# Rotary products on VectorE, branch B's scores evacuated at raised priority, and pair 1's raw columns in general slots

## The chip, the cores and the metric

The kernel runs on one core of a Trainium2 chip. The metric is the device time of one execution in microseconds (us). The engines are TensorE (PE: matmuls, and PEld: the loading of their weights), VectorE (DVE), ScalarE (ACT), GpSimd (POOL) and SyncE (SP), which starts most DMA transfers. Each engine works through its own queue in order, and an instruction that waits for another engine holds up all that stand behind it.

## The reference, cut to what matters

Two layers over 1024 tokens of width 1024, all in float32. A layer projects its normalised input with one wide matrix, whose columns feed three token mixers and their gates. Branch A is a gated multiplication over chunks of tokens, branch C an attention without softmax. Branch B, which the change touches, is an attention over a sliding window with rotary q and k; the gates of all branches come from the same projection:

```python
h = rms_norm(x, g_pre)
p = h @ w_in                      # 7936 columns: u_a v_a gate_a q_b k_b v_b gate_b ... merge_logits
...
def rope(x, pos):
    x1, x2 = xf[..., :half], xf[..., half:]
    out = jnp.concatenate([x1 * cos - x2 * sin, x2 * cos + x1 * sin], axis=-1)
...
# branch B, blocks of 128 queries, each against its own and the previous block of 128 keys
s = jnp.einsum('bnqgrd,bnkgd->bngrqk', qb, kb) * (Dh ** -0.5)
s = jnp.where(valid, s, NEG)
p = jax.nn.softmax(jnp.concatenate([s, sink], axis=-1), axis=-1)[..., :-1]
o = jnp.einsum('bngrqk,bnkgd->bnqgrd', p, vb)
...
merged = gates_a * (y_a @ w_a) + gates_b * (y_b @ w_b) + gates_c * (y_c @ w_c)
x = x + rms_norm(merged @ w_out, g_post)
```

## The kernel before, in words

**Precision.** A float32 product is made of three matmuls on rounded operands (`mm3`, L128 to L130): each operand is split into a rounded part `hi` (ACT, L111) and a remainder `lo` (DVE, L112). A weight tile of 128 columns gives one cast `whi` (L111) and one subtraction `wlo` (L112) over 128x1024 elements.

**Order of the work.** The order on PE is that of the program, written out by hand. A list of projection jobs (`stream`) is dealt out in portions: `fill(us)` puts about so many microseconds of it between the steps of an attention, `need(label)` runs the list up to a job. The other engines' queues are set by a scheduler that takes the ready instruction of the highest priority; a block under `tc.high_priority()` goes ahead of work written before it. Tiles of 128x1024 live in 27 general slots, handed out first in, first out (`new`, `done`): a new tile waits for whatever still reads the slot's last tile. The numbers behind a name are slot and tile (s17_2701 is tile 2701 in slot 17).

**Branch B.** Columns of k (`kb`) and of four pairs of query heads (`qb0` to `qb3`) are projected in two halves each, evacuated by ACT (L279) and rotated (`rope`, L282): four transfers of 128 KB make a copy `sw` with halves exchanged (L292), POOL multiplies `sw` by sin (L293) and the tile `t` by cos (L294), DVE adds (L295). The result is split again (`after_q`: ACT L346, DVE L347, twice each). `scores(v)`, v from 0 to 7 and two for each query pair, makes 16 matmuls (L486) into two PSUM tiles `pz`, evacuates these by ACT (L492, L493, L498), a select on POOL (L494) and copies under a mask on DVE (L496, L499), and does the softmax: maximum (L503), small operations on 128x8 values (L504, L505, L509, L510), eight exponentials (ACT, L507) and a product (L511). The pool `pz` has two buffers, so the next `scores` waits for the evacuation of the last. Behind it stand transposes (L519, split by ACT L111 and DVE L112), selects (POOL, L526) and the product with v (L543, evacuated by ACT L553 and DVE L554). Before the first scores `fill(14)` stands, before the second `fill(3)`, before the loop `fill(FB[0])`; each step of the loop has more of them (FB[1] to FB[5]). The gate tiles of branch B (b0 to b3) are among the jobs dealt out; ACT takes the first half of each out of PSUM (L257), DVE the second (L253), into a general slot.

**Dense.** After the attentions the remaining projections run as block products with seven multiplications for a pair of column tiles (`dense`, L719). `begin(p)` loads the raw columns of pair p (two loads of 512 KB, L778), `prep(p)` makes seven operands `wop` of them (splits L111/L112, sums on POOL L751 to L762), `prod` multiplies. In odd pairs from the third on the raw columns stand in two general slots, in all others, pair 1 among them, in the two buffers of the pool `wr`, which the jobs' weights and pair 0 use as well. Branch A's normalisation (L615 to L621 on DVE) is issued at the start of `dense`.

Of the kernel before, what the change touches and what calls it, by code (L numbers as in the profile page):

```python
# [19 lines left out]
ALU = mybir.AluOpType  # L20
AX = mybir.AxisListType

P = 128
# [6 lines left out]
NEG = -1e30  # L30
# [3 lines left out]
O_M = 4864  # L34
NSLOT = 27
FC = (0.6, 0.6, 1.2, 0.6)
FB = (4, 1.5, 1.5, 1.8, 2.4, 2.4)
FB_MORE = {1: 2.3, 2: 1.3}


# [1 line left out]
def trunk(ctx, tc, x, w_in, gm_w_s, gm_b_s, gm_g, sinks, w_ba, w_bb, w_bc, b_merge, w_out,  # L42
          g_pre, g_post, cos_t, sin_t, out):
    nc = tc.nc
# [15 lines left out]
    def new(dt=F32):  # L60
        i = free.popleft()
        t = sp.tile([P, 1024], dt, name=f"s{i}", tag=f"s{i}", bufs=1)
        held[id(t)] = (i, t)
        return t

    def done(*ts):
        for t in ts:
            free.append(held.pop(id(t))[0])
# [72 lines left out]
    def step():  # L141

        while stream:
            j = stream[0]
            if j.gen is None:
                if j.w is None:
                    j.w = j.load()
                j.gen = j.run(j.w)
                if len(stream) > 1:
                    stream[1].w = stream[1].load()  # L150
            c = next(j.gen, None)
            if c is not None:
                for d in list(deferred):
                    d[0] -= c
                    if d[0] <= 0:
                        deferred.remove(d)
                        d[1]()
                return c
            finished.add(j.label)
            stream.popleft()  # L160
        return None

    def fill(us):
        while us > 0:
            c = step()
            if c is None:
                return
            us -= c

    def need(label):  # L170
        while label not in finished:
            assert step() is not None, label
# [72 lines left out]
    def queue_layer(l, S):  # L245
# [38 lines left out]
        def rope(t):  # L284
            if "cos" not in S:
                S["cos"], S["sin"] = new(), new()
                nc.sync.dma_start(S["cos"], cos_t)
                nc.sync.dma_start(S["sin"], sin_t)
            sw = new()
            for a in range(4):  # L290
                b = a ^ 1
                nc.sync.dma_start(sw[a * 32:(a + 1) * 32, :], t[b * 32:(b + 1) * 32, :])  # L292
            nc.gpsimd.tensor_tensor(sw, sw, S["sin"], op=ALU.mult)  # L293
            nc.gpsimd.tensor_tensor(t, t, S["cos"], op=ALU.mult)  # L294
            nc.vector.tensor_tensor(t, t, sw, op=ALU.add)  # L295
            done(sw)

# [173 lines left out]
    def branch_b(l, S):  # L471
        def scores(v):
            hp, nh = divmod(v, 2)
            grp = hp // 2
            need(("qb", hp))
            qT, kk = S["qs", hp], S["kk"][grp]
            s = new()
            s3 = s.rearrange("p (c k) -> p c k", c=8)
            for q in range(2):
                z = pz().rearrange("p (c k) -> p c k", c=4)  # L480
                for j in range(2):
                    n = nh * 4 + q * 2 + j
                    k0 = max(n - 1, 0) * P
                    for e in range(2):
                        for i in range(2):
                            nc.tensor.matmul(z[:, e * 2 + j], qT[e][:, n * P:(n + 1) * P], kk[i][:, k0:k0 + 256],  # L486
                                             start=i == 0, stop=i == 1)
                sq = s3[:, q * 4:(q + 1) * 4]
                mp = mprev.bitcast(I32).unsqueeze(1)
                if nh == 0 and q == 0:  # L490

                    nc.scalar.copy(sq[:, 0::2], z[:, 0::2, :P])  # L492
                    nc.scalar.copy(sq[:, 1::2], z[:, 1::2, P:])  # L493
                    nc.gpsimd.affine_select(sq[:, 0::2], sq[:, 0::2], pattern=[[0, 2], [-1, P]], compare_op=ALU.is_ge,  # L494
                                            fill=NEG, base=0, channel_multiplier=1)
                    nc.vector.copy_predicated(sq[:, 1::2], mp.to_broadcast([P, 2, P]), z[:, 1::2, :P])  # L496
                else:
                    nc.scalar.copy(sq, z[:, :, P:])  # L498
                    nc.vector.copy_predicated(sq, mp.to_broadcast([P, 4, P]), z[:, :, :P])  # L499
            mx = sm.tile([P, 8], F32, name="mx", tag="mx", bufs=3)  # L500
            ls = sm.tile([P, 8], F32, name="ls", tag="ls", bufs=3)
            es = sm.tile([P, 8], F32, name="es", tag="es", bufs=3)
            nc.vector.tensor_reduce(mx, s3, axis=AX.X, op=ALU.max)  # L503
            nc.vector.scalar_tensor_tensor(mx, mx, -1.0, nsnk8[:, l * 4 + hp], op0=ALU.mult, op1=ALU.min)  # L504
            nc.vector.tensor_tensor(es, mx, snk8[:, l * 4 + hp], op=ALU.add)  # L505
            for c in range(8):
                nc.scalar.activation(s3[:, c], s3[:, c], AF.Exp, bias=mx[:, c:c + 1], accum_out=ls[:, c:c + 1])  # L507
            nc.scalar.activation(es, es, AF.Exp)
            nc.vector.tensor_tensor(ls, ls, es, op=ALU.add)  # L509
            nc.vector.reciprocal(ls, ls)  # L510
            nc.vector.tensor_tensor(s3, s3, ls.unsqueeze(2).to_broadcast([P, 8, P]), op=ALU.mult)  # L511
            if nh:
                done(*qT)
            return s
# [44 lines left out]
                done(o)  # L559

        need(("qb", 0))
        fill(14)
        ready = {0: scores(0)}
        fill(3)
        ready[1] = scores(1)
        fill(FB[0])
        pend = None
        for v in range(8):
# [8 lines left out]
            if v >= 6:  # L577
                S["T"].go(3)
            fill(FB[1])
            if pend:  # L580
                attend(*pend)
            fill(FB[2])
            s = ready.pop(v)
            p0 = transp(s, 0)
            fill(FB[3] + FB_MORE.get(v, 0))
            p1 = transp(s, 1)
            done(s)
            if v >= 6:
                S["T"].go(3)
            fill(FB[4])  # L590
            attend(v, 0, p0, o)
            fill(FB[5])
            pend = (v, 1, p1, o)
# [125 lines left out]
    def dense(l, S):  # L719
# [45 lines left out]
        def begin(p):  # L765

            if p < len(pairs) and p not in begun:
                begun.add(p)
                raws[p] = ([], [])
                for q in range(2):  # L770
                    if p % 2 and p > 2:
                        t = new()
                        raws[p][1].append(t)
                        t = t.rearrange("p (k c) -> p k c", k=4)
                    else:
                        t = wp.tile([P, 4, 256], F32, name="wr", tag="wr", bufs=2)
                    col = pairs[p][0]
                    nc.sync.dma_start(t, w_in[l, q * 512:(q + 1) * 512, col:col + 256]  # L778
                                      .rearrange("(k p) c -> p k c", p=P))
                    raws[p][0].append(t)  # L780
# [303 lines left out]
    with tc.manual_schedule(engines={mybir.EngineType.PE}):  # L1084
# [3 lines left out]
        for l in range(L):  # L1088
            S = states[l]
# [49 lines left out]
```

## Time and profile before

| | us |
|---|---|
| median of 3 executions (2069.59 to 2070.36) | 2069.74 |
| the profiled execution | 2070.14 |
| its span, from the first instruction to the last | 2068.4 |
| PE busy | 2015.1 (97%) |
| DVE busy | 1227.0 (59%) |
| ACT busy | 808.3 (39%) |
| POOL busy | 504.3 (24%) |
| mean granted clock of PE | 0.989 of full speed |

The profiled execution lies 0.4 us above the median. Its time is 1.74 us more than its span, which is the time around the first and the last instruction. Busy times are sums over the span; a matmul's duration overlaps the next one's start, so the spacing of starts tells the pace of PE, not the durations. The granted clock is given as a share of 2.4 GHz, so 0.50 is 1.2 GHz. Times in the rows count from the start of the span.

### The profile page before, as it was taken

What the parts mean: (1) busy time and instruction counts of PE and PEld (TensorE: products, weight loads), DVE (VectorE), ACT (ScalarE), POOL (GpSimd) and SP (SyncE); (2) the same over time, 40 slices, a digit from 0 to 9 for tenths busy, and PEclk for the clock granted to TensorE, in tenths of its full rate; (3) what the DMA queues carried; (4) which work ended last, traced back from release to release, by engine and by line L of the source; (5) the groups of instructions that cost most, each with busy time, mean ns of one, the idle gap of its engine ahead of it and who ended that gap; (6) DMA issues with size and microseconds to landing.
All of it is one profiled execution on the core that took longest, in us unless ns stands there. A gap on an engine that the chain in (4) does not pass through costs nothing.

```text
span 2068.4 us, 26597 instructions
## 1 busy us (share of the span) xinstructions
PE 2015.1 (97%) x10193; PEld 1688.1 (82%) x10193; DVE 1227.0 (59%) x1609; ACT 808.3 (39%) x1477; POOL 504.3 (24%) x501
## 2 busy tenths in 40 slices
PE   7999998999999999999999999989989999999998
PEld 7898886897888888888898888779978888888886
DVE  5565638567676666554546565576766666655533
ACT  6344436543234434212444344455423343432221
POOL 0221223132433220151002222231344222202500
PEclk9999998999999999999999999989999999999999
DMA  7111232223466546632441112222235655476213
GB/s 237 39 42 42 82 82 72 88 82 116 156 232 202 178 138 244 232 124 92 135 130 31 42 41 83 75 78 101 89 99 201 226 186 169 152 254 224 82 52 132
DMA packets 169055, 261.81 MB, mean 127 GB/s; under 512 B 8616, under 2 KB 122336, under 8 KB 168928
## 3 DMA queue, kind: packets, MB, share of 16 engines
q1 hardware_dynamic: 162016, 234.95, 35.0%
q10 hardware_dynamic: 6912, 25.17, 3.0%
q8 instruction: 80, 1.31, 0.3%
q14 instruction: 47, 0.39, 0.1%
HBM read 175.15 MB, written 79.69 MB: 123 GB/s over the span
## 4 chain that ended last, share of the span: by engine, by line
PE 87%; DVE 6%; ACT 3%; issue 2%; POOL 1%; DMA 1%; SPq 0%; DVEq 0%; POOLq 0%; ACTq 0%
PE pj L130 16%; PE pj L129 16%; PE pj L128 16%; PE pz L130 6%; PE pz L128 5%; PE pz L129 5%; PE ptr L130 5%; PE ptr L128 5%; PE ptr L129 5%; PE ptr L413 1%; PE pz L486 1%; PE pav L543 1%; PE pav L129 1%; DVE s L112 1%; PE pav L130 1%
## 5 line engine op out<-in xcount | busy, mean ns | idle before, releaser
L128 PE MATMUL pj<-h,whi 128*128 128x512 f32 x700 | 287.1, 410 | 9.2 <-ACT s L257 9.2
L129 PE MATMUL pj<-h,whi 128*128 128x512 f32 x700 | 279.1, 399 | 0.0
L130 PE MATMUL pj<-h,wlo 128*128 128x512 f32 x700 | 278.6, 398 | 0.0
L128 PEld LDWEIGHTS pj<-h,whi 128*128 128x128 f32 x700 | 133.6, 191 | 35.0 <-ACT s L257 10.1
L130 PEld LDWEIGHTS pj<-h,wlo 128*128 128x128 f32 x700 | 132.9, 190 | 32.0
L129 PEld LDWEIGHTS pj<-h,whi 128*128 128x128 f32 x700 | 133.3, 190 | 23.5
L112 DVE TENSOR_TENSOR wlo<-wr,whi 128x1024 fp32r<-128x1024 f32 x80 | 107.0, 1340 | 72.2 <-ACT whi L111 72.1
L128 PE MATMUL pj<-whi,h 128*128 128x256 f32 x512 | 148.5, 290 | 1.2 <-ACT h L111 1.2
L111 ACT CAST whi<-wr 128x1024 fp32r<-128x1024 f32 x80 | 84.0, 1050 | 159.8 <-PE pj L129 104.1
L130 PE MATMUL pj<-whi,h 128*128 128x256 f32 x512 | 144.4, 282 | 1.8 <-DVE h L112 1.8
L129 PE MATMUL pj<-wlo,h 128*128 128x256 f32 x512 | 144.1, 281 | 0.1
L940 POOL TENSOR_TENSOR s<-s,s 128x512 f32<-128x512 f32 x56 | 81.4, 1457 | 223.8 <-DVE s L934 197.9
L111 ACT CAST wop<-wr 128x512 fp32r<-128x512 f32 x120 | 73.1, 617 | 149.6 <-DMA wr<-in_w_in_dram 34.5
L112 DVE TENSOR_TENSOR wop<-wr,wop 128x512 fp32r<-128x512 f32 x120 | 101.4, 848 | 41.9 <-ACT wop L111 41.7
L396 DVE TENSOR_TENSOR_SCAN s<-s,ones 128x128 f32<-128x128 f32 (+3 forms) x64 | 87.6, 1369 | 63.5 <-POOL s L391 63.3
L111 ACT CAST wop<-s 128x512 fp32r<-128x512 f32 x118 | 71.9, 618 | 122.2 <-PE pz L130 43.7
L112 DVE TENSOR_TENSOR s<-ptr,s 128x512 fp32r<-128x512 f32 (+2 forms) x132 | 77.2, 589 | 66.5 <-ACT s L111 66.0
L112 DVE TENSOR_TENSOR wop<-s,wop 128x512 fp32r<-128x512 f32 x118 | 97.8, 834 | 12.2 <-ACT wop L111 11.8
L129 PE MATMUL pj<-h,s 128*128 128x512 f32 x256 | 102.0, 398 | 0.0
L128 PE MATMUL pj<-h,s 128*128 128x512 f32 x256 | 101.1, 395 | 0.0
L130 PE MATMUL pj<-h,s 128*128 128x512 f32 x256 | 100.6, 393 | 0.0
L130 PEld LDWEIGHTS pj<-whi,h 128*128 128x128 f32 x512 | 97.1, 190 | 2.7 <-DVE h L112 2.7
(230 smaller groups left out, 5176.9 us busy)
## 6 DMA issues: line engine op xcount, KB each, us to landing
wr<-in_w_in_dram SPq DMA_DIRECT2D x96, 512.0 KB, 4.0
sg<-s ACTq DMA_DIRECT2D x48, 512.0 KB, 5.1
s<-sg SPq DMA_DIRECT2D x48, 512.0 KB, 4.9
s<-in_w_in_dram SPq DMA_DIRECT2D x28, 512.0 KB, 5.1
s<-in_x_dram SPq DMA_DIRECT2D x16, 512.0 KB, 4.1
hT<-s SPq DMA_DIRECT2D x16, 512.0 KB, 3.2
s<-hT SPq DMA_DIRECT2D x16, 512.0 KB, 3.8
wor<-in_w_out_dram SPq DMA_DIRECT2D x16, 512.0 KB, 3.7
```

Of the source, the lines that this page charges most:

```text
L111: nc.scalar.copy(hi, raw)
L112: nc.vector.tensor_tensor(lo, raw, hi.bitcast(F32), op=ALU.subtract)
L128: nc.tensor.matmul(acc, lh, rh, start=first, stop=False)
L129: nc.tensor.matmul(acc, lh, rl, start=False, stop=False)
L130: nc.tensor.matmul(acc, ll, rh, start=False, stop=last)
L396: nc.vector.tensor_tensor_scan(t1[:, :kl][:, ::-1], t1[:, :kl][:, ::-1], ones.to_broadcast([P, kl]), 1.0, op0=ALU.mult, op1=ALU.mult)
L413: nc.tensor.transpose(pt[:, b - b0], t2[:, b * P:(b + 1) * P], ident)
L486: nc.tensor.matmul(z[:, e * 2 + j], qT[e][:, n * P:(n + 1) * P], kk[i][:, k0:k0 + 256], start=i == 0, stop=i == 1)
L543: nc.tensor.matmul(av[:, j], w, t.rearrange("p (e j) k -> p e j k", j=2)[:, :, j], start=i == 0, stop=i == len(ops) - 1)
L940: eng.tensor_tensor(acc[dm][:, ts], acc[dm][:, ts], sg[:, ts], op=ALU.add)
```

## The change

Three edits. In `rope` the two products move from POOL to DVE, and the one by cos, which doesn't need the exchanged copy, comes first; there are five ropes in a layer. In branch B the evacuation of the scores is put under `tc.high_priority()`, and the portions between its steps are set anew: 12, 5 and 5 ahead of the first, second and third scores in place of 14, 3 and 4, and 1.4, 1.4, 1.7, 2.2, 2.2 inside the loop in place of 1.5, 1.5, 1.8, 2.4, 2.4. In `dense` the raw columns of pair 1 stand in two general slots too. Lines from L490 on have a number higher by one in the changed kernel.

```diff
-FB = (4, 1.5, 1.5, 1.8, 2.4, 2.4)
+FB = (5, 1.4, 1.4, 1.7, 2.2, 2.2)
...
-            nc.gpsimd.tensor_tensor(sw, sw, S["sin"], op=ALU.mult)
-            nc.gpsimd.tensor_tensor(t, t, S["cos"], op=ALU.mult)
+            nc.vector.tensor_tensor(t, t, S["cos"], op=ALU.mult)
+            nc.vector.tensor_tensor(sw, sw, S["sin"], op=ALU.mult)
             nc.vector.tensor_tensor(t, t, sw, op=ALU.add)
...
-                if nh == 0 and q == 0:
+                with tc.high_priority():
+                    if nh == 0 and q == 0:
...
-                else:
-                    nc.scalar.copy(sq, z[:, :, P:])
-                    nc.vector.copy_predicated(sq, mp.to_broadcast([P, 4, P]), z[:, :, :P])
+                    else:
+                        nc.scalar.copy(sq, z[:, :, P:])
+                        nc.vector.copy_predicated(sq, mp.to_broadcast([P, 4, P]), z[:, :, :P])
...
-        fill(14)
+        fill(12)
         ready = {0: scores(0)}
-        fill(3)
+        fill(5)
...
-                    if p % 2 and p > 2:
+                    if p % 2:
```

Three places of the new order. The first is DVE in layer 1 where qb0 is rotated (`t` is s17_2701, `sw` is s9_2742, s10 and s12 hold cos and sin) and its split begins (L347). Before:

```order
L112 TENSOR_TENSOR wlo_2832<-wr_2829,whi_2831 128x1024
L295 TENSOR_TENSOR s17_2701<-s17_2701,s9_2742 128x1024
L112 TENSOR_TENSOR wlo_2991<-wr_2988,whi_2990 128x1024
L347 TENSOR_TENSOR s16_2750<-s17_2701,s16_2750 64x1024
L347 TENSOR_TENSOR s8_2751<-s17_2701,s8_2751 64x1024
L496 COPY_PREDICATED s13_2857<-mprev_79,pz_2858 128x2x128
L499 COPY_PREDICATED s13_2857<-mprev_79,pz_2873 128x512
```

and with the change:

```order
L112 TENSOR_TENSOR s4_2660<-s20_2629,s4_2660 128x8x64
L293 TENSOR_TENSOR s17_2701<-s17_2701,s10_2574 128x1024
L294 TENSOR_TENSOR s9_2742<-s9_2742,s12_2575 128x1024
L112 TENSOR_TENSOR wlo_2991<-wr_2988,whi_2990 128x1024
L295 TENSOR_TENSOR s17_2701<-s17_2701,s9_2742 128x1024
L347 TENSOR_TENSOR s16_2750<-s17_2701,s16_2750 64x1024
L347 TENSOR_TENSOR s8_2751<-s17_2701,s8_2751 64x1024
L497 COPY_PREDICATED s13_2848<-mprev_79,pz_2849 128x2x128
L500 COPY_PREDICATED s13_2848<-mprev_79,pz_2864 128x512
```

Two products come in, and the subtraction wlo_2991, which needs the cast of a weight tile on ACT (whi_2990), now stands between them and the addition L295 instead of behind it.

The second is DVE up to the rotation of qb3 (t is s22_3065, sw is s16_3115), on which the tile waits that takes the first half of gate tile b0 (pj_3147 before, pj_3135 now) out of PSUM. Before, this tile is s22_3227, in the slot of the rotated tile, whose last reader is the second L347:

```order
L295 TENSOR_TENSOR s22_3065<-s22_3065,s16_3115 128x1024
L112 TENSOR_TENSOR s9_3241<-ptr_3236,s9_3241 128x512
L554 TENSOR_TENSOR s0_3004<-pav_3210,s16_3219 64x256
L509 TENSOR_TENSOR ls_3184<-ls_3184,es_3185 128x8
L510 RECIPROCAL ls_3184<-ls_3184 128x8
L347 TENSOR_TENSOR s8_3123<-s22_3065,s8_3123 64x1024
L554 TENSOR_TENSOR s0_3004<-pav_3210,s16_3219 64x256
L347 TENSOR_TENSOR s5_3124<-s22_3065,s5_3124 64x1024
```

With the change it is s16_3213, in the slot of the exchanged copy, whose last reader is the addition L295:

```order
L347 TENSOR_TENSOR s7_2982<-s23_2905,s7_2982 64x1024
L347 TENSOR_TENSOR s2_2983<-s23_2905,s2_2983 64x1024
L500 COPY_PREDICATED s13_3163<-mprev_79,pz_3164 128x512
L555 TENSOR_TENSOR s0_3007<-pav_3139,s23_3146 64x256
L500 COPY_PREDICATED s13_3163<-mprev_79,pz_3175 128x512
L555 TENSOR_TENSOR s0_3007<-pav_3139,s23_3146 64x256
L512 TENSOR_TENSOR s20_3008<-s20_3008,ls_3036 128x1024
L293 TENSOR_TENSOR s22_3065<-s22_3065,s10_2574 128x1024
L294 TENSOR_TENSOR s16_3115<-s16_3115,s12_2575 128x1024
L504 TENSOR_REDUCE mx_3186<-s13_3163 128x8
L112 TENSOR_TENSOR s9_3244<-ptr_3239,s9_3244 128x512
L295 TENSOR_TENSOR s22_3065<-s22_3065,s16_3115 128x1024
```

The tile is now free at an earlier instruction, and the two products stand ahead of it in the same queue.

The third is SP where the loads of pair 1 are started (wr_4494 and wr_4496 before). Before:

```order
L778 DMA wr_4400<-in_w_in_dram 128x4x256
L558 DMA ob0_88<-s2_3653 128x1024
L607 DMA s6_4455<-in_gm_w_s_dram 128x4x128
L681 DMA s13_4418<-hT0_93 128x2x512
L681 DMA s2_4426<-hT0_93 128x2x512
L558 DMA ob0_88<-s8_4049 128x1024
L603 DMA s8_4453<-in_gm_b_s_dram 128x512
L778 DMA s22_4769<-in_w_in_dram 128x4x256
L778 DMA wr_4494<-in_w_in_dram 128x4x256
L840 DMA gc0_86<-s4_4500 128x1024
L778 DMA wr_4496<-in_w_in_dram 128x4x256
```

and with the change (s3_4494 and s14_4496):

```order
L779 DMA wr_4379<-in_w_in_dram 128x4x256
L559 DMA ob0_88<-s2_3656 128x1024
L608 DMA s6_4455<-in_gm_w_s_dram 128x4x128
L779 DMA s14_4496<-in_w_in_dram 128x4x256
L682 DMA s13_4397<-hT0_93 128x2x512
L682 DMA s2_4405<-hT0_93 128x2x512
L779 DMA s3_4494<-in_w_in_dram 128x4x256
L559 DMA ob0_88<-s8_4040 128x1024
L604 DMA s8_4453<-in_gm_b_s_dram 128x512
```

The loads of pair 1 stand ahead of the last output of branch B now, and before they stood behind the loads of a later pair's slot and, the second one, behind a store of pair 0's result.

## Rows read from the trace of the kernel before

**Rows 1.** The view of all waits of TensorE (PE) over the whole span: the line that waited, the engine and line that it waited for, microseconds in total, number of times, the longest.

```profile
PE pj L128 <- ACT s L257: 9.2, 2, 4.9
...
PE pz L486 <- DVE s L499: 8.1, 2, 4.1
...
PE ptr L130 <- DVE wop L112: 5.3, 2, 3.0
PE pj L130 <- DVE wop L112: 2.9, 2, 2.4
PE pz L130 <- DVE wop L112: 2.7, 2, 2.2
```

**Rows 2.** The timeline of PE around two scores of branch B, layer 1. Columns: start, duration, engine, line, operation, output and inputs, partitions x elements, count, and in brackets the idle time before it and its releaser. Each L486 row is one call of `scores`, 16 matmuls.

```profile
307.47 2.08 PE L486 MATMUL pz<-s,s 128*128 128x256 f32 x16
309.39 0.39 PE L128 MATMUL pj<-h,whi 128*128 128x512 f32 x1
...
310.08 0.39 PE L128 MATMUL pj<-h,whi 128*128 128x512 f32 x1
...
323.91 3.78 PE L486 MATMUL pz<-s,s 128*128 128x256 f32 x16 [4.07 <-DVE s L499]
327.48 0.63 PE L128 MATMUL pj<-h,whi 128*128 128x512 f32 x1
...
330.04 0.40 PE L128 MATMUL pj<-h,whi 128*128 128x512 f32 x1
```

**Rows 3.** The view by windows, same part of layer 1. Columns: window, its length, busy time and instructions of PE, PEld, DVE, ACT and POOL, then the granted clock of PE, the share of the DMA engines and GB/s.

```profile
300.00:320.00 20.00, 19.84 (x101) 16.41 (x99) 12.36 (x12) 10.99 (x23) 7.18 (x4) 1.00 0.21 54
324.00:330.00 6.00, 6.00 (x22) 5.47 (x23) 6.00 (x7) 1.96 (x7) 3.54 (x3) 0.50 0.35 98
330.00:354.00 24.00, 23.96 (x124) 19.77 (x122) 20.62 (x27) 17.47 (x63) 11.45 (x9) 1.00 0.31 88
```

**Rows 4.** The timeline of PE at the first matmul of gate tile b1 (layer 1), whose PSUM buffer held the first half of gate tile b0; columns as in rows 2. The second row is the first matmul that starts at the old spacing again.

```profile
358.33 0.80 PE L128 MATMUL pj<-h,whi 128*128 128x512 f32 x1 [4.37 <-ACT s L257]
...
364.33 0.40 PE L128 MATMUL pj<-h,whi 128*128 128x512 f32 x1
```

**Rows 5.** The timeline of PE in the first two pairs of `dense`: two waits of layer 1, each with the first matmul that starts at the old spacing again, and the longest wait of layer 2.

```profile
486.17 0.50 PE L130 MATMUL ptr<-h,wop 128*128 128x512 f32 x1 [2.24 <-DVE wop L112]
...
490.61 0.40 PE L130 MATMUL pz<-h,wop 128*128 128x512 f32 x1
...
495.94 0.49 PE L130 MATMUL pj<-h,wop 128*128 128x512 f32 x1 [2.37 <-DVE wop L112]
...
500.85 0.40 PE L129 MATMUL ptr<-s,wop 128*128 128x512 f32 x1
...
1517.95 0.79 PE L130 MATMUL ptr<-h,wop 128*128 128x512 f32 x1 [3.02 <-DVE wop L112]
...
1521.42 0.40 PE L129 MATMUL ptr<-h,wop 128*128 128x512 f32 x1
```

**Rows 6.** The timelines of POOL and of DVE (VectorE) in layer 1, where branch B's first tiles are rotated and their softmax begins: a product of a rope on POOL, then on DVE the rope's addition, small operations of the softmax, and one evacuation under the mask.

```profile
299.63 2.41 POOL L294 TENSOR_TENSOR s<-s,s 128x1024 f32<-128x1024 f32 x1
...
311.81 2.40 POOL L294 TENSOR_TENSOR s<-s,s 128x1024 f32<-128x1024 f32 x1
...
302.07 1.22 DVE L295 TENSOR_TENSOR s<-s,s 128x1024 f32<-128x1024 f32 x1 [8.43 <-POOL s L294]
...
310.20 0.75 DVE L499 COPY_PREDICATED s<-mprev,pz 128x512 f32<-128x512 int32 x1 [0.45 <-ACT s L498]
...
312.31 1.92 DVE L504 SCALAR_TENSOR_TENSOR mx<-mx,nsnk 128x8 f32<-128x8 f32 x1
...
332.76 0.17 DVE L504 SCALAR_TENSOR_TENSOR mx<-mx,nsnk 128x8 f32<-128x8 f32 x1
```

**Rows 7.** The timelines of ACT (ScalarE) and DVE from the end of qb0's rotation to the first scores, layer 1.

```profile
302.54 1.06 ACT L111 CAST whi<-wr 128x1024 fp32r<-128x1024 f32 x1 [4.77 <-PE pj L129]
...
303.98 2.11 ACT L346 CAST s<-s 64x1024 fp32r<-64x1024 f32 x2
...
303.63 1.23 DVE L112 TENSOR_TENSOR wlo<-wr,whi 128x1024 fp32r<-128x1024 f32 x1 [0.33 <-ACT whi L111]
305.06 2.47 DVE L347 TENSOR_TENSOR s<-s,s 64x1024 fp32r<-64x1024 f32 x2 [0.20 <-ACT s L346]
```

**Rows 8.** The timeline of ACT at the evacuation of the first half of gate tile b0, layer 1.

```profile
357.69 0.59 ACT L257 COPY s<-pj 128x512 f32<-128x512 f32 x1 [0.70 <-DVE s L347]
```

**Rows 9.** The timelines of SP (the queue that starts the loads), ACT and DVE where `dense` begins, layer 1: the two loads of pair 1, the first rounding of each, and the remainders (`wop`) made from them.

```profile
478.18 0.38 SPq L778 DMA_DIRECT2D wr<-in_w_in_dram  x1
...
486.17 0.37 SPq L778 DMA_DIRECT2D wr<-in_w_in_dram  x1
...
481.91 0.62 ACT L111 CAST wop<-wr 128x512 fp32r<-128x512 f32 x1 [9.37 <-DMA wr<-in_w_in_dram]
...
489.94 0.62 ACT L111 CAST wop<-wr 128x512 fp32r<-128x512 f32 x1 [3.41 <-DMA wr<-in_w_in_dram]
...
485.46 0.65 DVE L112 TENSOR_TENSOR wop<-wr,wop 128x512 fp32r<-128x512 f32 x1
...
490.74 4.54 DVE L621 TENSOR_SCALAR s<-s,mv,rs 128x512 f32<-128x512 f32 x7
495.21 1.28 DVE L112 TENSOR_TENSOR wop<-wr,wop 128x512 fp32r<-128x512 f32 x2
```

More of the change, by code (lines that the diff above doesn't have):

```diff
@@ L489, in scores @@
                 mp = mprev.bitcast(I32).unsqueeze(1)
-                if nh == 0 and q == 0:
[L492 to L496, printed above, removed]
-                else:
-                    nc.scalar.copy(sq, z[:, :, P:])
-                    nc.vector.copy_predicated(sq, mp.to_broadcast([P, 4, P]), z[:, :, :P])
+                with tc.high_priority():
+                    if nh == 0 and q == 0:
+                        nc.scalar.copy(sq[:, 0::2], z[:, 0::2, :P])
+                        nc.scalar.copy(sq[:, 1::2], z[:, 1::2, P:])
+                        nc.gpsimd.affine_select(sq[:, 0::2], sq[:, 0::2], pattern=[[0, 2], [-1, P]], compare_op=ALU.is_ge,
+                                                fill=NEG, base=0, channel_multiplier=1)
+                        nc.vector.copy_predicated(sq[:, 1::2], mp.to_broadcast([P, 2, P]), z[:, 1::2, :P])
+                    else:
+                        nc.scalar.copy(sq, z[:, :, P:])
+                        nc.vector.copy_predicated(sq, mp.to_broadcast([P, 4, P]), z[:, :, :P])
             mx = sm.tile([P, 8], F32, name="mx", tag="mx", bufs=3)
```

## The prediction

> **What bounds the kernel now.** PE is busy 97% of the span, so the first view to read is PE's own waits [rows 1], and the question for each is what ended last there. Three kinds matter. The first is the third call of branch B's scores, which waits for the second call's evacuation on DVE (L486 on L499, 8.1 us in two layers). The second is the first matmul of gate tile b1, which waits until ACT has taken gate tile b0 out of its PSUM buffer (L128 on L257, 9.2 us); that copy was itself held up by DVE, whose L347 ended only then [rows 8]. The third is the start of `dense`, where PE waits for DVE's `wop` remainders (5.3 + 2.9 + 2.7 us).
>
> Next the timelines, for what a wait costs behind itself. After the 4.07 us wait, 16 score matmuls take 327.48 - 323.91 = 3.57 us where they took 309.39 - 307.47 = 1.92, and the six behind them 2.56 where three took 0.69, so 1.40 for six [rows 2]: 1.65 + 1.16 = 2.8 us on top. The windows show why: granted clock 0.50 (1.2 GHz) there, 1.00 (2.4 GHz) before and behind [rows 3]. After the 4.37 us wait, twelve matmuls and four transposes take 6.00 us; at the old spacing twelve take 2.80, and four transposes I estimate at 0.09 each, so the price is 2.85 [rows 4]. In `dense`, 13 matmuls take 4.44 us after the 2.24 us wait (3.03 at the old spacing), 14 take 4.91 after the 2.37 one (3.27), and 9 take 3.47 after layer 2's wait of 3.02 (2.10) [rows 5]: 1.4, 1.6 and 1.4 us.
>
> Loss in layer 1: branch B 4.07 + 2.8 + 4.37 + 2.85 = 14.1; `dense` 0.45 + 2.24 + 1.4 + 2.37 + 1.6 = 8.1 (0.45 is what rows 1 leave beside a 2.24 wait on the line L130 of pz, 2.7 - 2.24). Layer 2 has the same waits, the second of branch B 4.9 and the last of `dense` 3.02: 14.6 and 0.55 + 2.24 + 1.4 + 3.02 + 1.4 = 8.6 (0.55 = 2.9 - 2.37). **Together 45.4 us** is the most that the change can win.
>
> **Rope products on DVE.** A product on POOL takes 2.41 us, an addition of the same shape on DVE 1.22 [rows 6], so DVE takes over 10 x 1.22 = 12.2 us a layer and POOL gives up 24. DVE has a return: operations on 128x8 values, 0.17 us when free, take 1.92 when they meet a POOL product, ending just when the product ends (312.31 + 1.92 against 311.81 + 2.40) [rows 6]. Four such meetings in a layer at some 1.75 us are 7 us, so DVE's net load is about +5 us a layer, and only where PE waits for DVE does it count. For kb I count nothing: it is rotated ahead of qb0, with qb0's and qb1's projections still to run on PE.
>
> A rule of the Trainium skill (SBUF — State Buffer, "Who interferes with whom") bears on this: a DVE operation with two SBUF inputs and a GpSimd operation that reads SBUF exclude each other for the whole instruction. L504's row agrees. The rule also speaks against the change, since every product on DVE can now hold up POOL's selects (L494, L526); by it a select ahead of a maximum starts up to one product later, 1.2 us, and if that reached PE in each layer the sum would be 2.4 us worse.
>
> **The first scores: a new wait.** Before, POOL's products end at 302.04, L295 runs at 302.07, L346 at 303.98, L347 at 305.06 to 307.53, and PE reaches the scores at 307.47 with no idle time [rows 2, 6, 7]. Two things change. Fewer fills (12 for 14, three steps of three matmuls) bring PE there nine matmuls earlier, at 307.47 - 9 x 0.233 = 305.37. And on DVE the subtraction `wlo` now stands ahead of L295. It needs a cast on ACT that waits for PE to leave a weight buffer (302.54, 4.77 idle), so it can't start before 303.63 [rows 7]; the products themselves are done long before and gain nothing. L295 then starts at 303.63 + 1.2 = 304.8, the first L346 (1.05) at 306.05, the first L347 (1.23) at 307.2 to 308.45, the second at 309.65. PE waits 3.05 us, does two matmuls, waits 1 more: **4.1 us a layer** where there was none. Behind this wait are queued only PE's own matmuls; ACT and DVE wait for the scores. Its clock price: between 1.4 (after 3.02) and 2.8 (after 4.07). I take 1.4, since it is a wait of 3 and one of 1, and the sub-microsecond waits cost no clock; both ends stay in the range.
>
> **The third scores.** From the first scores to the third PE has 32 score matmuls and 48 others, 3.84 + 11.2 = 15.0 us. In that time DVE has at most 8 operations of 1.22, five evacuations of 0.75 or less and two small ones [rows 6]: some 14 us, of which it needs 10 before qb1 is split, and with raised priority the evacuation no longer stands behind exponentials on ACT and a softmax product on DVE. Waits shown on L499 therefore vanish with some 3 us to spare: **-4.07 - 2.8**.
>
> **Gate b0.** Its tile now waits for L295 of qb3 instead of a later L347, but in a longer queue. From the third scores' evacuation to that L295 DVE has 14 operations of 1.22 to 1.23, nine of 128x512 or less (0.75 at most, an estimate of 0.6 on average) and six small ones of 0.17: 17.2 + 5.4 + 1.0 = 23.6 us, 25.0 at most. It starts 310.20 - 307.47 = 2.7 us behind PE [rows 2, 6]; ACT's copy adds 0.59 [rows 8]. So the copy is done 26.9 to 28.3 us after PE starts those scores. PE has there 32 score matmuls, 84 projections and 26 short matmuls or transposes at about 0.12: 3.84 + 19.6 + 3.1 = 26.5. The wait is 0.4 to 1.8 us; I take **0.7**, without a clock price. If DVE idles somewhere on the way, it is more: that is the third rival. The new values of FB only shift PE's arrivals, and are in these counts.
>
> **Dense.** Before, pair 1's loads start at 478.18 and 486.17, when the `wr` buffers come free; their first casts wait for them to 481.91 and 489.94, and the remainders come at 485.46 and, behind 4.54 us of normalisation, 495.21, each a few tenths ahead of a PE wait's end [rows 5, 9]. In general slots the loads stand ahead of branch B's last output in SP's queue, so they start while its last attention runs; at 3.7 us for one (481.91 - 478.18) they are there before pair 0 begins. They move past two loads of hT for `dense`, which now stand behind the slot that pair 1's first load waits for. I cost that at nothing, since branch B's last attention and the filling behind it cover it; without that cover the sums from hT, and PE's products with them, would start later by such a wait. Then the remainders follow DVE's queue alone. There are still eight normalisation steps of 0.65 us (4.54 for 7) ahead of the third operand of pair 1, but the first two are made before them. With the longer filling of some 2 us at the end of branch B I reckon each operand ready within 0.3 us of its use: **0.5 a layer left of 8.1 and 8.6**. Bounds: nothing left, or all of it.
>
> **Sum.** Left in a layer: 4.1 + 1.4 + 0.7 + 0.5 = 6.7; both layers 13.4. The gain is 45.4 - 13.4 = 32.0. The profiled execution took 2070.14 us, of which 1.74 lies around the span; 2070.14 - 32.0 = 2038.1, and as the median of the runs is 0.4 lower, **2038 us**. PE's work is the same matmuls. Against 0.2% (4 us), which is about what a measurement of this kernel can tell from no change, this is a clear gain. With the other clock price and 1.8 at gate b0 it is 2043, with `dense` clean 2037.
>
> **Rivals.**
> (1) The first scores don't wait: the cast comes earlier, or DVE's addition is not held by it. For: only one cast stands in between. Against: that cast's row shows the wait for PE [rows 7]. 2 x 5.5 us better: 2027.
> (2) `dense` keeps its waits. For: DVE's normalisation stood ahead of `wop` before, and still stands ahead of the third operand. Against: the casts that waited for the transfer [rows 9]. 16.7 - 1.0 = 15.7 us worse: 2054.
> (3) DVE becomes the bound in branch B and gate b0's wait stays as it was with its clock, 4.4 + 2.85 for 0.7. For: 25 us of queue against 26.5 of PE leaves no room for idling, and ACT's exponentials feed that queue. Against: the returns above. 13 us worse: 2051.
> (4) Slower. All of DVE's new 12.2 us lands on the path in each layer, since qb1 to qb3 are rotated where PE has only one attention's work in hand, with the first wait at 4.1 + 2.8, while the old waits of branch B stay: 14.1 + 12.2 + 6.9 = 33.2 for 14.1, less 7.6 won in `dense`: 11.5 a layer, 2093. It turns from gain to loss where branch B's waits pass 14.1 + 7.6 = 21.7 us a layer.
>
> **How the numbers follow.** Forecast 0.62, rival 1 0.10, rival 2 0.09, rival 3 0.11, rival 4 0.05, and 0.03 for branch B giving up just what `dense` wins. The range from 2026 to 2054 takes in the forecast with both its bounds and the first three rivals. Faster 0.92, same 0.03, slower 0.05.
>
> **What would show it.** PE's waits of the changed kernel: a new one on DVE's L347 of 3 to 4 us at the first scores, at 305; none on L500 at the third; under 2 us on L257; no `wop` wait over 0.5. On DVE, the 128x8 operations at 0.17 throughout, and L295 of qb0 at 304.8, directly behind `wlo`. SP issuing both loads of pair 1 before 470. A wait of several microseconds on L257 proves rival 3, `wop` waits of 2 us rival 2, and I would be wrong altogether if new waits show in branch B beyond these, at transposes or at L543.

## The result, and the profile after

The changed kernel takes 2045.05 us (median; 2044.38 to 2045.31) against 2069.9 us for the kernel before in the same runs: ratio 0.9879, 95% interval 0.9867 to 0.9891, so 24.85 us faster. The forecast was 2038 with a range of 2026 to 2054: the direction and the range held, the gain was three quarters of the forecast 32. The profiled execution's span is 2043.5 us, its mean granted clock 0.997 (0.989 before).

All waits of TensorE by line, over the whole span, in the changed kernel (columns as in [rows 1]; lines after L490 are one higher):

```profile
PE pz L486 <- DVE s L347: 7.0, 4, 2.9
...
PE pj L128 <- ACT s L257: 1.9, 2, 1.0
...
PE pz L130 <- DVE wop L112: 1.7, 2, 1.3
PE ptr L520 <- DVE s L555: 1.7, 2, 0.8
PE pj L130 <- DVE wop L112: 1.3, 1, 1.3
...
PE ptr L130 <- DVE wop L112: 0.4, 1, 0.4
```

The row of L486 on L499 is gone, L257 went from 9.2 us to 1.9, and the three rows of `wop` from 10.9 to 3.4. Two rows are new: 7.0 us on L347, the wait at the first scores, and 1.7 us at a transpose of branch B (L520), which I had not seen coming.

The first scores, on PE (the timeline, layer 1, columns as in [rows 2]):

```profile
308.76 0.50 PE L486 MATMUL pz<-s,s 128*128 128x256 f32 x2 [2.91 <-DVE s L347]
310.01 3.13 PE L486 MATMUL pz<-s,s 128*128 128x256 f32 x14 [0.75 <-DVE s L347]
312.94 0.63 PE L128 MATMUL pj<-h,whi 128*128 128x512 f32 x1
...
313.77 0.40 PE L130 MATMUL pj<-h,wlo 128*128 128x512 f32 x1
```

and on DVE in the same stretch:

```profile
298.58 1.22 DVE L294 TENSOR_TENSOR s<-s,s 128x1024 f32<-128x1024 f32 x1
303.94 1.23 DVE L112 TENSOR_TENSOR wlo<-wr,whi 128x1024 fp32r<-128x1024 f32 x1 [4.14 <-ACT whi L111]
305.08 1.22 DVE L295 TENSOR_TENSOR s<-s,s 128x1024 f32<-128x1024 f32 x1
307.49 2.47 DVE L347 TENSOR_TENSOR s<-s,s 64x1024 fp32r<-64x1024 f32 x2 [1.19 <-ACT s L346]
```

The two products are done at 299.8, and the addition L295 stands behind `wlo`, which waits 4.14 us for its cast. L295 starts when `wlo` ends, at 305.08, and everything up to the scores follows from that. PE waits 2.91 and 0.75 us where it had waited for nothing [rows 2, 7], and its next 14 matmuls take 2.93 us where 14/16 of 1.92 is 1.68.

The windows of layer 1's branch B (columns as in [rows 3]):

```profile
312.00:318.00 6.00, 6.00 (x27) 5.02 (x26) 4.65 (x6) 1.31 (x3) 0.33 (x1) 0.86 0.00 0
318.00:348.00 30.00, 30.00 (x165) 25.70 (x164) 26.34 (x38) 23.68 (x72) 6.58 (x5) 1.00 0.32 89
348.00:366.00 18.00, 17.02 (x90) 14.08 (x89) 15.15 (x22) 11.40 (x31) 4.71 (x5) 1.00 0.17 59
```

The clock stands at 1.00 from 318 on; before, it was 0.50 behind the third scores [rows 3]. Both old losses of clock in branch B are gone, and one new one stands behind the first scores.

In `dense`, what became of [rows 5, 9] in layer 1, on PE:

```profile
472.63 0.50 PE L130 MATMUL pz<-s,wop 128*128 128x512 f32 x1 [1.29 <-DVE wop L112]
...
478.86 0.50 PE L130 MATMUL ptr<-h,wop 128*128 128x512 f32 x1 [0.39 <-DVE wop L112]
```

on POOL:

```profile
463.93 2.15 POOL L749 TENSOR_TENSOR s<-s 128x512 f32<-128x512 f32 x1 [8.84 <-DVE s L112]
466.16 2.15 POOL L751 TENSOR_TENSOR s<-s,s 128x512 f32<-128x512 f32 x1
```

and on DVE:

```profile
462.57 2.35 DVE L112 TENSOR_TENSOR s<-s,s 128x1024 fp32r<-128x1024 f32 x2
464.84 4.55 DVE L112 TENSOR_TENSOR h<-s,h 128x1024 fp32r<-128x1024 f32 x2
...
471.93 0.65 DVE L112 TENSOR_TENSOR wop<-wr,wop 128x512 fp32r<-128x512 f32 x1
```

Before, the wait of 0.45 us that [rows 1] left over stood at the same product as the 1.29 now, and these are ACT's casts of pair 0's last operands:

```profile
478.09 0.50 PE L130 MATMUL pz<-s,wop 128*128 128x512 f32 x1 [0.45 <-DVE wop L112]
```

```profile
465.12 0.62 ACT L111 CAST wop<-s 128x512 fp32r<-128x512 f32 x1
...
468.06 1.14 ACT L111 CAST wop<-wr 128x512 fp32r<-128x512 f32 x2
...
469.58 0.62 ACT L111 CAST wop<-wr 128x512 fp32r<-128x512 f32 x1
```

Taken product by product, waits of 0.45, 2.24 and 2.37 us have become 1.29, 0.39 and none. The 2.24 and the 2.37 had different causes, and [rows 9] reads one of them wrongly. An operand made from a general slot (`s`) is the fourth of its pair, so the cast at 469.58 is of pair 0's seventh and last operand, and the one at 481.91 is the first of pair 1. The remainders follow in the same order, so the one at 485.46, which ended the 2.24 us wait, is pair 0's last. Its cast had been done since 470.2 and no load was missing: it stood on DVE behind steps of the normalisation (L615, L616) and a sum of products (L818). Only the wait of 2.37 us (3.02 in layer 2), ended by the remainders at 495.21, is one of pair 1.

The wait of 1.29 us has a cause of its own: two remainders of `h` (L112) take 4.55 us, where two of the same size just ahead take 2.35. In that stretch POOL does pair 1's first two sums (L749 and L751, 2.15 us each). Before, the first of them ran at 481.99, in 1.29 us; the raw columns had landed only then [rows 9].

### The profile page after: what moved, and what is told of

Its sections match the earlier page's. It is cut to its first block, busy times and chain, and to the rows that moved or that the text cites. A ratio compares the mean times of both kernels' runs of the same rounds, so it can differ in the third digit from the quotient of the medians.

```text
span 2043.5 us, 26583 instructions
## 1 busy us (share of the span) xinstructions
PE 2004.6 (98%) x10193; PEld 1679.4 (82%) x10193; DVE 1240.7 (61%) x1629; ACT 808.0 (40%) x1477; POOL 466.6 (23%) x481
## 4 chain that ended last, share of the span: by engine, by line
PE 87%; DVE 7%; ACT 2%; issue 2%; POOL 1%; DMA 1%; SPq 0%; DVEq 0%; POOLq 0%; ACTq 0%
PE pj L128 16%; PE pj L129 16%; PE pj L130 16%; PE pz L130 6%; PE pz L129 6%; PE pz L128 6%; PE ptr L130 5%; PE ptr L128 5%; PE ptr L129 5%; PE pz L486 1%; PE ptr L413 1%; PE pav L129 1%; PE pav L544 1%; DVE s L112 1%; PE pav L130 1%
## 5 line engine op out<-in xcount | busy, mean ns | idle before, releaser
L112 DVE TENSOR_TENSOR wlo<-wr,whi 128x1024 fp32r<-128x1024 f32 x80 | 106.1, 1328 | 85.6 <-ACT whi L111 85.4
L111 ACT CAST wop<-s 128x512 fp32r<-128x512 f32 x130 | 78.7, 618 | 135.7 <-PE pz L130 45.6
L112 DVE TENSOR_TENSOR wop<-s,wop 128x512 fp32r<-128x512 f32 x130 | 108.1, 842 | 12.3 <-ACT wop L111 11.9
L112 DVE TENSOR_TENSOR wop<-wr,wop 128x512 fp32r<-128x512 f32 x108 | 93.7, 868 | 34.3 <-ACT wop L111 34.2
L112 DVE TENSOR_TENSOR s<-ptr,s 128x512 fp32r<-128x512 f32 (+2 forms) x132 | 77.3, 589 | 58.4 <-ACT s L111 57.5
L111 ACT CAST wop<-wr 128x512 fp32r<-128x512 f32 x108 | 66.0, 617 | 113.0 <-PE ptr L130 29.4
```

The lines of the kernel that those rows point to most:

```text
L111: nc.scalar.copy(hi, raw)
L112: nc.vector.tensor_tensor(lo, raw, hi.bitcast(F32), op=ALU.subtract)
```

## The experiments

Each was run against the kernel before, on the same chip; the medians of before were 2069.5, 2069.47 and 2070.47 us in the three groups (e1 to e4, e5 to e8, e9 to e11). Differences are taken within a group.

**e1: the products of rope alone on DVE**, all else as before.

```diff
-            nc.gpsimd.tensor_tensor(sw, sw, S["sin"], op=ALU.mult)
-            nc.gpsimd.tensor_tensor(t, t, S["cos"], op=ALU.mult)
+            nc.vector.tensor_tensor(t, t, S["cos"], op=ALU.mult)
+            nc.vector.tensor_tensor(sw, sw, S["sin"], op=ALU.mult)
```

> The kernel before with the products of rope on VectorE and nothing else. Theory (each wait of TensorE in branch B is set by VectorE's queue, and the products on GpSimd were a part of that queue's delay): the wait at the third scores shrinks from 4.07 us to 2 us or less a layer, a new wait of some 2 us comes at the first scores, gate tile b0's wait stays between 1 and 5 us, dense is unchanged; 2058 to 2066 us. Rival (VectorE's 12.2 us a layer land on the path, and only raised priority cures the third scores): 2072 us or more.

Measured: 2063.22 us, ratio 0.9974 (0.9965 to 0.9984), 6.3 less. PE's waits:

```profile
PE pj L128 <- ACT s L257: 12.4, 2, 6.2
...
PE pz L486 <- DVE s L347: 3.1, 4, 0.8
```

The third scores have no wait, as the theory says, but gate b0's wait grew from 4.37 to 6.18 us in layer 1 (4.86 to 6.18 in layer 2), more than the 1 to 5 that I had expected. A good part of what the products free at one place comes back at the next.

**e2: the priority and the portions alone** (products on POOL, pair 1 in `wr`).

```diff
-FB = (4, 1.5, 1.5, 1.8, 2.4, 2.4)
+FB = (5, 1.4, 1.4, 1.7, 2.2, 2.2)
...
+                with tc.high_priority():
+                    if nh == 0 and q == 0:
...
-        fill(14)
+        fill(12)
...
-        fill(3)
+        fill(5)
```

> The kernel before with the raised priority and the new portions, products on GpSimd, pair 1 in wr. Theory: the evacuation no longer stands behind the softmax product, and the third scores come 2 us later, so their wait goes without the move of the products: no wait there, none at the first scores (the addition stands ahead of the weight's remainder in VectorE's order), gate tile b0's wait stays at 2 to 4 us, dense unchanged; 2053 to 2061 us. Rival (the third scores wait for GpSimd's products): within 3 us of before.

Measured: 2047.84 us, ratio 0.9895 (0.9879 to 0.9912), 21.7 less, more than I had expected of it. No wait is left at the third scores, and gate b0's wait is 1.6 us. The first scores wait 0.79 + 0.76, where I had expected none, and the 2.24 us of `dense` have become 0.38 in layer 1 and nothing in layer 2. The second edit alone brings most of the change.

**e3: the general slots alone.**

```diff
-                    if p % 2 and p > 2:
+                    if p % 2:
```

> The kernel before with pair 1's raw columns in two general slots and nothing else. Theory: the waits of dense go from 8.1 and 8.6 us a layer with their clock to some 1.5, as in the changed kernel; 2056 to 2058 us, branch B's waits unchanged at 4.07 and 4.4. GpSimd's first two sums for pair 1 come early and meet VectorE's remainders of h, which then take 2.2 us and not 1.2. Rival (the longer filling ahead of dense and not the slots gave the gain): less than 5 us of gain.

Measured: 2061.14 us, ratio 0.9965 (0.9952 to 0.9978), 8.4 less; I had expected 12 to 13. Branch B's waits are as before. In `dense` two new waits come on the remainders of `h`, and 2.24 us on `wop` is left in each layer:

```profile
PE pz L130 <- DVE wop L112: 2.8, 2, 2.2
PE ptr L130 <- DVE wop L112: 2.2, 1, 2.2
...
PE ptr L129 <- DVE h L112: 1.5, 1, 1.5
PE pz L129 <- DVE h L112: 1.2, 1, 1.2
```

So the slots take away the waits at pair 1's operands and not the 2.24 us at pair 0's last one; that goes with the new portions (e2, e10), and that part of the rival is right. The clock is 1.00 behind these 2.24 us (484 to 494 in layer 1), where 1.4 us were lost before.

**e4: the changed kernel with one weight's split behind qb0's.** It takes the remainder from ahead of L295, and its cast from ahead of qb0's casts on ACT.

```diff
+        if k == KD and len(adds) % 5 == 4:
+            with tc.issue_after(adds[-3].ins), tc.issue_after(casts[-5].ins):
+                split(hi, lo, raw)
+        else:
+            split(hi, lo, raw)
...
+            adds.append(nc.vector.tensor_tensor(t, t, sw, op=ALU.add))
...
+                casts.append(nc.scalar.copy(q[src], t[src]))
```

> The changed kernel with one weight's split put behind qb0's: its cast behind qb0's two casts on ScalarE, its remainder behind the addition on VectorE. Theory (the new wait of 2.9 + 0.75 us at the first scores is that remainder, which waits for TensorE through its cast): the wait falls to about 2 us in two pieces, without a clock price, 6 to 7 us less in all: 2038 to 2040 us. Rival (ScalarE's evacuation of qb1, which ends only then, holds the casts all the same): 2044 to 2046.

Measured: 2036.02 us, ratio 0.9839 (0.9825 to 0.9854): 33.5 less than before, where the changed kernel has 24.9 less. On DVE, then on PE:

```profile
300.06 1.23 DVE L300 TENSOR_TENSOR s<-s,s 128x1024 f32<-128x1024 f32 x1
304.90 2.47 DVE L352 TENSOR_TENSOR s<-s,s 64x1024 fp32r<-64x1024 f32 x2 [3.61 <-ACT s L351]
307.40 1.23 DVE L113 TENSOR_TENSOR wlo<-wr,whi 128x1024 fp32r<-128x1024 f32 x1
```

```profile
306.17 0.51 PE L491 MATMUL pz<-s,s 128*128 128x256 f32 x2
307.43 1.93 PE L491 MATMUL pz<-s,s 128*128 128x256 f32 x14 [0.75 <-DVE s L352]
```

The addition now follows the products at 300.06, the remainder comes behind the split, and of 2.91 + 0.75 us only 0.75 is left. The theory holds, and its size was larger than I had written. The edit moves the remainder and its cast together; which of the two counts more was not run.

**e5: the changed kernel with the products back on POOL** (the reverse of e1's diff).

> The changed kernel with the products of rope back on GpSimd. Theory now (the move of the products costs as much as it brings, since it puts a weight's remainder ahead of qb0's addition): waits at the first scores 0.8 + 0.75 us without a clock price, gate tile b0 and two products with v wait 1.5 us each, dense as in the changed kernel: 2038 to 2042 us, less than the changed kernel. Rival (what I predicted from: the products on VectorE take waits away and are worth it): 2048 us or more.

Measured: 2044.19 us, ratio 0.9877 (0.9862 to 0.9891), as fast as the changed kernel within the intervals. The theory's waits are there (0.8 + 0.75 at the first scores, 1.6 at gate b0, 0.8 and 1.5 at products with v), its time is 2 us off; the rival falls. Some of that is clock: the theory gave the first scores' waits no clock price, but in layer 2 of this trace the clock fell behind them (0.72 from 1315 to 1321), which cost 1.6 us. In the change as it stands, the move of the products is worth nothing that can be measured.

**e6: pair 1's first two sums on DVE.**

```diff
-            nc.gpsimd.tensor_tensor(s3, a11, a21, op=ALU.subtract)
+            eng = nc.vector if p == 1 else nc.gpsimd
+            eng.tensor_tensor(s3, a11, a21, op=ALU.subtract)
...
-            nc.gpsimd.tensor_tensor(a21, a21, a22, op=ALU.add)
+            eng.tensor_tensor(a21, a21, a22, op=ALU.add)
```

> The changed kernel with pair 1's first two sums (of each layer) on VectorE in place of GpSimd. Theory (pair 1's early sums on GpSimd meet VectorE's remainders of h, 4.55 us for two, and that makes the 1.3 us wait of dense): the two remainders take 2.4 us again, the wait falls to 0.5 or less: 2042 to 2044 us. Rival (VectorE's queue is what holds the remainder, and two more sums in it lengthen the wait): 2045 or more.

Measured: 2046.92 us, ratio 0.989 (0.9875 to 0.9905). On DVE, then on PE:

```profile
464.33 2.35 DVE L112 TENSOR_TENSOR h<-s,h 128x1024 fp32r<-128x1024 f32 x2
...
479.60 3.29 DVE L622 TENSOR_SCALAR s<-s,mv,rs 128x512 f32<-128x512 f32 x7
482.79 0.69 DVE L752 TENSOR_TENSOR s<-s,s 128x512 f32<-128x512 f32 x1
```

```profile
485.60 0.50 PE L128 MATMUL ptr<-s,wop 128*128 128x512 f32 x1 [1.24 <-ACT wop L111]
...
486.85 0.79 PE L130 MATMUL ptr<-s,wop 128*128 128x512 f32 x1 [0.53 <-DVE wop L112]
```

The mechanism is shown: without POOL's sums the two remainders of `h` take 2.35 us, and in layer 1 the waits of 1.29 and 0.39 are gone (in layer 2 the 0.39 is left). The time did not follow and came out where the rival had it, since the second sum now stands behind seven steps of the normalisation and the operands made from it come late (1.24 and 0.53 us on PE, and in layer 1 the clock falls behind them, 0.72 from 486 to 492).

**e7: the changed kernel without the raised priority.**

> The changed kernel without the raised priority of the scores' evacuation. Theory (the portions and the move of the products cure the third scores, as the run with the products alone had no wait there): within 2 us of the changed kernel, 2043 to 2047. Rival (the raised priority is what cures them): a wait of 2 to 4 us at the third scores with its clock, 2052 or more.

Measured: 2050.61 us, ratio 0.991 (0.9895 to 0.9925), 18.9 less than before, so about 6 us of the gain of 24.85 hang on the priority. The third scores wait 2.33 us again (the theory said none). The rival had the place right and the price too high: no clock was lost behind this wait in either layer (1.00 from 326 to 336 and from 1340 to 1350).

**e8: the changed kernel with the portions of before.**

> The changed kernel with the portions of before (14, 3, 4 and 1.5 to 2.4). Theory (the portions bring TensorE 2.1 us earlier to the first scores and 2 us more filling ahead of dense): the wait at the first scores falls to about 1.5 us without a clock price, 3.7 us less a layer, and dense loses 2 to 3 us a layer: 2041 to 2045. Rival (the portions carry the gain in branch B): 2050 or more.

Measured: 2055.13 us, ratio 0.993 (0.9913 to 0.9946), 14.3 less than before. The theory fails, the rival holds. The wait at the first scores falls to 0.81 + 0.75 us a layer as expected, but:

```profile
PE pj L128 <- ACT s L257: 8.3, 2, 4.2
...
PE pz L130 <- DVE wop L112: 2.8, 2, 2.2
PE ptr L130 <- DVE wop L112: 2.2, 1, 2.2
```

gate b0's wait is back at 4.2 us a layer, with its loss of clock, and so are 2.2 us of `dense`. And in layer 1 the clock fell behind the first scores' short waits as well, for which the theory had no price; the last section shows it.

**e9: e4, and pair 1's first two sums on DVE at raised priority.**

```diff
+            if p == 1:
+                with tc.high_priority():
+                    nc.vector.tensor_tensor(s3, a11, a21, op=ALU.subtract)
+                    nc.vector.tensor_tensor(a21, a21, a22, op=ALU.add)
```

> The split put behind qb0's and, on top, pair 1's first two sums on VectorE at raised priority, so that they don't stand behind the normalisation. Theory (the wait of dense is the meeting of GpSimd's sums with VectorE's remainders of h; the run with the sums on VectorE lost only because they came late): waits in dense fall from 1.3 + 0.4 to 0.5 or less a layer and no new one comes: 2033 to 2035 us, the fastest so far. Rival (VectorE has no room in dense): 2037 or more.

Measured: 2034.64 us, ratio 0.9829 (0.9815 to 0.9844), the fastest of all, though its interval overlaps e4's (0.9825 to 0.9854). The wait of 1.28 falls to 0.45, but the next one on `wop` grows from 0.38 to 1.11: the theory's time came, its waits did not.

**e10: the portions alone**, all else as before.

> The kernel before with the portions alone. Theory (TensorE's later arrival at the third scores takes up half of their wait, the raised priority the other half, and the longer filling helps dense): 1.5 to 2 us of wait at the third scores, waits of dense as in the run with priority and portions: 2050 to 2057 us. Rival (the portions are all of it): 2046 to 2049.

Measured: 2047.56 us, ratio 0.9896 (0.988 to 0.9913), 22.9 less: the rival. PE's waits, and the window of layer 1's branch B:

```profile
PE pj L128 <- ACT s L257: 3.5, 2, 1.8
...
PE pav L543 <- DVE s L112: 2.4, 2, 1.2
...
PE pz L486 <- DVE s L499: 1.6, 2, 0.8
```

```profile
300.00:366.00 66.00, 60.31 (x311) 49.62 (x311) 50.07 (x60) 40.04 (x111) 26.14 (x19) 1.00 0.28 80
```

The waits have not gone: in layer 1 they are 0.79 + 0.76 at the first scores, 0.79 at the third, 1.74 at gate b0, 0.44 and 1.17 at products with v, 5.7 us where 4.07 + 4.37 = 8.4 were, and 0.83 more come at a late transpose. But none is longer than 1.8 us, and the clock is 1.00 throughout. By these waits about half of the gain is branch B's and the other half is in `dense`: there layer 1 has one wait of 2.77 us and no loss of clock, where 8.1 us went before, and layer 2 has 1.24 + 0.53 and a loss of some 1.6 where 8.6 went. The edit moves matmuls behind the first scores and lengthens the filling ahead of `dense`; the two were not run apart.

**e11: e4 with the products on POOL.**

> The split put behind qb0's, with the products of rope on GpSimd. Theory (the move of the products is worth what it takes at gate b0 and at two products with v, 3 us a layer, once it no longer delays qb0): 2041 to 2043 us, 5 to 7 us more than with the products on VectorE. Rival (the split alone made the difference and the move is worth nothing): 2036 to 2038.

Measured: 2043.11 us, ratio 0.9869 (0.9854 to 0.9884), against 2036.02 for e4. With qb0's addition free of the weight's remainder, the move of the products is worth 6 to 7 us; the rival falls.

| kernel | products on DVE | priority | portions | slots | split behind | us less than before |
|---|---|---|---|---|---|---|
| e1 | yes | | | | | 6.3 |
| e10 | | | yes | | | 22.9 |
| e3 | | | | yes | | 8.4 |
| e2 | | yes | yes | | | 21.7 |
| e5 | | yes | yes | yes | | 25.3 |
| e7 | yes | | yes | yes | | 18.9 |
| e8 | yes | yes | | yes | | 14.3 |
| changed kernel | yes | yes | yes | yes | | 24.9 |
| e11 | | yes | yes | yes | yes | 27.4 |
| e4 | yes | yes | yes | yes | yes | 33.5 |

The parts don't add: three of them alone give 6.3 + 22.9 + 8.4 = 37.6. Not in the table are e6 (22.6 less) and e9 (35.8 less), which also move pair 1's sums.

## Why the prediction was right, and where its sizes were off

**Losses before.** Branch B and `dense` lost what the rows said. In layer 1, where I had the rows, the gain follows from them: 14.1 + 8.1 less what is left, 2.91 + 0.75 + 1.6 (clock) + 0.97 + 0.83 + 1.29 + 0.39 = 8.7, gives 13.5, and PE reached branch A's transposes 13.0 us earlier than before, counted from the first transposes of branch C. In layer 2 I had put the same clock prices of 2.8 and 2.85 behind its waits, and they were smaller there: in the trace of before the 16 scores and three matmuls behind its third scores lose 1.66 + 0.56 = 2.2 us, and the stretch behind its gate wait 2.3. That is 1.15 us too much in the 45.4.

**First scores: right.** Forecast 4.1 us in two pieces, with 1.4 of clock; measured 3.66 and 1.6 in layer 1, 3.36 and some 2.6 in layer 2. The cause, `wlo` with its cast ahead of qb0's split, is shown by e4. My worry in rival 1 that the wait might not come was wrong.

**Third scores: the wait went, but not for one reason.** I gave it to the priority together with the products. Portions alone bring it to 0.79 (e10), products alone to none (e1), and with products and portions but no priority it is 2.33 (e7). No single edit was necessary for most of it, so the number was right and its reason only in part.

**Gate b0: right.** Forecast 0.7 us, measured 0.97, and without a loss of clock. Rival 3 had no room in the change, but it is what e8 and e1 show (4.2 and 6.2 us): the queue of DVE between the third scores and qb3's addition does fill PE's time there, and the portions decide. I had written of them that they "only shift PE's arrivals". That is true and was the main thing: nine matmuls (2.1 us) moved from ahead of the first scores to behind them, so every later use in branch B lies 2.1 us further behind the softmax work that it waits for.

**Dense: mis-sized, and one cause read wrongly.** I put both long waits of layer 1 down to pair 1's loads. The 2.24 us one was pair 0's last operand in DVE's queue: the slots leave it (e3, e8), and it fell to 0.39 because the portions were changed as well. That it went was partly luck: my reason for it was wrong, and the new portions, whose longer filling I had counted only as a help, did it. The term "0.5 a layer left" measured 1.68. The loads came as early as forecast (444.03 and 455.57), but I did not ask what they would set off: POOL's sums started at once and met DVE's remainders of `h` (e6). The rule of the Trainium skill that the prediction weighed (SBUF — State Buffer, "Who interferes with whom": two such operations exclude each other for the whole instruction) was the right one at the wrong place. The trace agrees, with 4.55 us for two remainders beside POOL's sums and 2.35 without. Its cost in branch B is visible and small, in `dense` it made a wait of 1.3 us a layer out of 0.45 and 0.55.

**Not foreseen:** 0.83 us a layer at a late transpose of branch B (L520 on L555, at 434.83 in layer 1), with no loss of clock. It stands in every run with the new portions (e2, e5, e10 as well) and in none without, so it belongs to them. New waits at transposes were what I had named as the sign of being wrong altogether; one came, and it was too small for that.

**Short waits at no price: not so in every execution.** I wrote that sub-microsecond waits cost no clock. At the single short waits of before and of the change it holds, but behind the first scores' 0.8 + 0.75 us it failed in layer 1 of e8 and in layer 2 of e2 and e5.

Of the 7 us between 32.0 and 24.9, `dense` is 2.4, L520 1.7, layer 2's clock prices before 1.15, the first scores' wait less 1.2 and its clock plus 1.4, gate b0 0.5: 6.0 in all. About 1 us stays without a row.

## What to carry to other kernels

Where an engine's clock falls behind a long wait, shorter pieces of idle time were cheaper here: in e10's branch B, layer 1, 6.5 us in pieces of under 2 us cost no clock, where two waits of 8.4 us together had cost 5.65 on top. It is no rule, since such pieces did cost clock in other runs. So before you speed up the late engine, try moving some of the waiting engine's own work from ahead of the chain's start to behind it. Read for each wait which operand ended it before you name its cause: two waits on the same line of `dense` had different ones, and different edits cured them. A step that starts earlier runs beside other work than before, so look for what its engine shares with those new neighbours. And when an operation changes engines, read the new queue around it: here a single weight remainder ahead of it took back all that the move was worth, and one order constraint gave it back.

## What the runs showed of the hardware

POOL and DVE held each other up in both directions. In the changed kernel POOL's select took 1.40 us where it takes 0.41 alone, and of DVE's 128x8 operations, 0.16 here, three a layer were held to between 0.53 and 0.60 (the one shown ends with a select that ran from 352.16 to 353.72):

```profile
311.92 0.41 POOL L495 TENSOR_SCALAR_AFFINE_SELECT s<-s 128x256 f32<-128x256 f32 x1 [61.11 <-ACT s L493]
327.99 1.40 POOL L495 TENSOR_SCALAR_AFFINE_SELECT s<-s 128x256 f32<-128x256 f32 x1 [15.66 <-ACT s L493]
```

```profile
318.95 0.16 DVE L505 SCALAR_TENSOR_TENSOR mx<-mx,nsnk 128x8 f32<-128x8 f32 x1
...
353.14 0.59 DVE L505 SCALAR_TENSOR_TENSOR mx<-mx,nsnk 128x8 f32<-128x8 f32 x1
```

The clock behind a wait did not follow from the wait's length alone. Behind waits of 4.07 us and more in branch B it was 0.50 for some microseconds each time. Below that both occur. Waits of 0.81 + 0.75 us at layer 1's first scores cost nothing in e1 (clock 1.00 from 307 to 312), but in e8 the clock was 0.66 from 308 to 313, and the 14 matmuls behind them, here for e1 and then for e8, took over a microsecond longer:

```profile
309.20 1.93 PE L486 MATMUL pz<-s,s 128*128 128x256 f32 x14 [0.75 <-DVE s L347]
```

```profile
309.25 3.30 PE L486 MATMUL pz<-s,s 128*128 128x256 f32 x14 [0.75 <-DVE s L347]
```

The wait of 2.24 us in `dense` cost 1.4 us before [rows 5] and nothing in e3, and 2.33 us at e7's third scores cost nothing. At the same place of layer 1's `dense`, TensorE waited 2.75 us in e2 and 2.77 in e10, and the windows behind (columns as in [rows 3]) are, for e2 and then for e10:

```profile
484.00:493.00 9.00, 6.95 (x18) 5.50 (x19) 6.78 (x9) 3.28 (x6) 2.25 (x2) 0.62 0.38 120
```

```profile
484.00:492.00 8.00, 5.53 (x25) 4.50 (x26) 7.23 (x10) 3.29 (x6) 2.69 (x2) 1.00 0.24 68
```

So a forecast that prices the clock behind waits of 2 to 3 us is off by up to 3 us for each, and one that puts shorter waits at nothing can be off by 1.6. The profiled execution of e2, 2050.61 us, is the longest of its four, whose median is 2047.84, so its trace stands for that execution and not for all. Nothing in these runs ties the loss to the priority, in which alone e2 and e10 differ, and that limits what the 1.2 us between their medians say of it. What else decides, these runs don't say.
